# Two more experts in fixed places, a 4 KB descriptor scratch and three more weight buffers in a hybrid GLA, pooling and mixture-of-experts layer

## The chip, the cores and the metric

The kernel runs on one core of a Trainium2 chip. The metric is the device time of one execution in microseconds; a kernel is timed in several runs and the median is compared. Lower is better.

## The reference: what is computed

One transformer layer over 1024 latent tokens of width 1024 with a 256-token context prefix: a modulated RMSNorm, a combined projection into gated linear attention and a pooling branch, an output projection with a gated residual, then a mixture of experts with a gated residual, and a final RMSNorm. What matters here is the mixture of experts. Each token picks one of 4 groups and in it the best 2 of 8 experts:

```python
pg = softmax(t @ w_rg); gp, gi = top_k(pg, 1)                 # one of 4 groups
le = take(t @ w_re, gi); ew, ei = top_k(softmax(le), 2)       # two of its 8 experts
gates = gp * ew / sum(ew)                                     # scattered to (32 experts, tokens)
y = sum_e (silu(t @ wi_a[e]) * (t @ wi_u[e])) @ wo[e] * gates[e][:, None]
```

All is float32. An expert's weights are 1024x512 and 256x1024 (3 MB), 32 experts are 96 MB; 1024 tokens make 2048 (token, expert) pairs.

## The kernel before, in words

**Stages.** Up to about 430 us of the trace come the modulation, the projections, the attention and the pooling (lines 300 to 1057). From line 1266 to 1402 follow the second half of the output projection (`out1_in` and its neighbours), the residual, the norm, and beside them the router (`route`, `counts`, `place`, `tables`). Each finished tile of the normed tokens is stored to `h2_d` in DRAM (L1299), each tile of the residual stream to `x2_d` (L1278). From line 1407 on come the experts, and at the end the last expert block is added on chip to the reloaded residual, normed and stored (L1798 to L1858).

**Blocks.** Every expert gets a number of rows (`CAPS`, by its rank among the experts sorted by load), and experts are put together into blocks of at most 128 rows (`unit`, L1712): 64+64, 96+32 and 64+48 rows from two experts, or 112 to 128 rows of one. There are 19 units and one `merged` block that holds what the two largest experts have over 128 rows, and the smallest's rows. Tokens that fit nowhere would go through a loop after the end (L1861), whose number of turns is read on the chip.

**Fixed places.** The last `NS` experts (26 to 31 before) have no rank by load but a fixed place, 64 rows each, in the first `NS/2` units, so that their weights can be asked for before the router has finished. The other experts' numbers (`eid`) are known only when `order_tables` (L1435) has run; `part` (L1701) reads them into a register of SyncE (`sy.value_load`).

**One block** (class `Block`, L1573): GpSimd gathers its rows from `h2_d` with an indirect DMA for each part (L1590), TensorE transposes them (L1611) and runs the first product (L1626, 8 steps of 128), ScalarE and VectorE apply the gate (L1632, L1633), TensorE transposes (L1639) and runs the second product (L1650), VectorE multiplies by the gates into `y` (L1655), and GpSimd adds `y` into `x2_d` with an accumulating indirect DMA for each part (`scatter`, L1668). All scatters write the same DRAM tensor, so each one waits until the one before it has landed. `y` has two buffers. TensorE's order is written out by hand (L1741 to L1780): the first product of unit n+1, the transposes of unit n+2, then the second product of unit n. `ORDER` is the order of the units.

**Weights.** A weight load is 512 KB into one slab of [128, 1024] floats; an expert needs 4 slabs for the first product and 2 for the second, 192 loads in all, issued by SyncE (L1254). Slabs are taken in turn from the list `slabs` (`next_slab`, L1246), a ring of 39 that reuses the memory of earlier stages: the chunk states (`dS`, `St`), the token buffers (`hall`), a table (`cs`), `wx`, `wraw`, `mix`, `hl`, the weights of the output projection (`woh`, `wol`) and `wz`. A load waits until its slab's last reader is done. SyncE's order isn't written by hand: a list scheduler puts an instruction ahead of others in program order when those aren't ready, so that a load whose slab is free early is issued early.

**The end** (L1782 to L1858). The last unit isn't scattered. When all scatters have landed, SyncE loads `x2_d` into eight slabs `y1` (L1802), TensorE adds the last block's rows by selection matrices `sel` (tag `hl`) from `yp` (tag `wraw`), and the tiles are normed and stored. `fgb`, `y1` and `jk` are the next slabs of the ring.

**GpSimd's scratch.** The program object is made with the default size of GpSimd's DMA descriptor scratch, 16 KB of each SBUF partition.

Of the kernel before, what the change touches and what calls it, by code (L numbers as in the profile page):

```python
# [19 lines left out]
P = 128  # L20
# [4 lines left out]
E = 32  # L25
EPS = 1e-6
NX = 28
NS = 6
ND = E - NS
NP, NA, NQ, NG = NS // 2, 4, 5, 5  # L30
C_X = NS
C_A = C_X + NA
C_B = C_A + NA
# [3 lines left out]
C_Y = C_D + 2  # L37
U_A, U_C, U_S, U_D = NP, NP + NA, NP + NA + NQ, NP + NA + NQ + NG
U_Y = U_D + 2
CAPS = [64] * NS + [32] * 5 + [48] * 5 + [64] * 5 + [80] + [96] * 3 + [112] * 2 + [128] * 3 + [P + 32, P + 64]  # L40
PLACES = [*range(NS), *range(NS, NS + 4), *range(NS + 15, NS + 19), *range(NS + 5, NS + 10),
          *range(NS + 14, NS + 9, -1), *range(NS + 19, E), NS + 4]
ORDER = [0, 1, 2, 13, 3, 14, 7, 15, 4, 8, 17, 18, 5, 9, 12, 10, 16, 6, 11]
NDB = 2
N_W1 = 2
N_W2 = 3
NXB = 3
# [26 lines left out]
def constants():  # L74
# [21 lines left out]
    c[:, O_TOK] = np.arange(P) + 1.0  # L96
    c[:, O_RK:O_RK + E] = PLACES
    c[:, O_CP:O_CP + E] = [CAPS[r] for r in PLACES]
    c[:, O_X:O_X + NX] = np.arange(NX)[None, :]
# [32 lines left out]
def hybrid_layer(ctx, tc, x, c, ctx_in, c_ctx, w_ada, b_ada, norm1_g, w_in, w_decay, b_decay, gla_norm_g,  # L132
                 w_pool, pool_scale, w_out, norm2_g, w_rg, w_re, w_e_in, w_e_out, final_g, cst_d, inv_d, out):
    nc = tc.nc
# [10 lines left out]
    out = out[0]  # L145

    const = ctx.enter_context(tc.tile_pool(name="const", bufs=1))
    dram = ctx.enter_context(tc.tile_pool(name="scratch", bufs=1, space=DRAM))

    kvb_d = [dram.tile([P, 1280], F32, name=f"kvb_d{i}") for i in range(NT)]  # L150
# [9 lines left out]
    cs = early.tile([P, D], F32, name="cs")  # L160
# [33 lines left out]
    def split(hi, lo, src, en=ve):  # L194
        sc.activation(hi, src, AF.Copy)  # L195
        en.tensor_tensor(lo, src, hi.bitcast(F32), OP.subtract)  # L196
# [32 lines left out]
    def mix(i):  # L229
        return mixs[i // 4][:, i % 4]  # L230
# [3 lines left out]
    wst = main  # L234
# [65 lines left out]
    with tc.tile_pool(name="pp", bufs=2) as pp, \  # L300
            tc.manual_schedule(engines={mybir.EngineType.PE, mybir.EngineType.DVE, mybir.EngineType.Activation}):
        xts, wa, wraw, wph, wpl = {}, {}, {}, {}, {}
# [294 lines left out]
    for j in range(5):  # L597
        t = wst.tile([P, D], F32, name="wraw", tag="wraw", bufs=2)
# [51 lines left out]
    St = sd.tile([P, 2, H, P], F32, name="St")  # L650
# [32 lines left out]
    with tc.tile_pool(name="kv", bufs=2) as kv:  # L683
# [115 lines left out]
        with tc.manual_schedule(engines={mybir.EngineType.PE}):  # L799
            k_proj(0, range(8))  # L800
            decay_in(0)
            for n in range(10):
# [18 lines left out]
                if n == 8:  # L821
                    wq, q_steps = load_split(kvw, [(0, 256)], "wk", en=gp)
# [22 lines left out]
    hslab = [hflat[:, j * D:(j + 1) * D] for j in range(10)]  # L845
# [222 lines left out]
    w1p = ctx.enter_context(tc.tile_pool(name="w1p", bufs=1, side="right"))  # L1068
# [165 lines left out]
    def slab(pool, tag, bufs=1):  # L1234
        return pool.tile([P, D], F32, name=tag, tag=tag, bufs=bufs)

    sds = [dS[:, 2 * j:2 * j + 2].rearrange("p i h e -> p (i h e)") for j in range(5)]
    slabs = [sds[4], St.rearrange("p a h e -> p (a h e)"), sds[0], hslab[3], sds[1], *hslab[4:6], sds[2], *hslab[6:8],
             sds[3], *hslab[8:10], cs]
    slabs += [slab(w1p, f"wx{j}") for j in range(N_W1)] + [slab(wst, "wraw", 2) for j in range(2)]  # L1240
    slabs += [mix(j).rearrange("p k n -> p (k n)") for j in range(NT)]
    slabs += [slab(wst, "hl", 2) for j in range(2)]

    ring = [0]

    def next_slab():  # L1246
        ring[0] += 1
        return slabs[(ring[0] - 1) % len(slabs)]

    def wslab(src):  # L1250
# [184 lines left out]
    def order_tables():  # L1435
# [17 lines left out]
        for lo, c in ((0, C_C), (64, C_B)):  # L1453
            c += ORDER[-1] - U_C
            te.matmul(h[lo:lo + 64], lhsT=tT[:, 0, 0:64], rhs=M[:, c:c + 1], start=True, stop=True)
# [13 lines left out]
    def extra_blocks():  # L1469
# [24 lines left out]
        ve.tensor_tensor(er[:, 2], incl, nx, OP.subtract)  # L1494
        ve.tensor_scalar(incl, incl, float(NDB), None, op0=OP.add)
        ve.tensor_copy(nxm, incl[:, E - 1:E])
# [28 lines left out]
        ve.tensor_tensor(poff, poff, fl, OP.add)  # L1525
        ve.scalar_tensor_tensor(poff, poff, float(NDB - 1 + 100), tm, op0=OP.add, op1=OP.mult)
        yield
# [4 lines left out]
        ve.tensor_tensor(slot, slot, q, OP.add)  # L1532
        ve.scalar_tensor_tensor(prk, prk, float(100 - (E - NDB)), sec, op0=OP.add, op1=OP.mult)
        ve.scalar_tensor_tensor(xb, poff, -100.0, prk, op0=OP.add, op1=OP.add)
# [32 lines left out]
        ve.tensor_copy(tab[:, :, 2].bitcast(F32), wtab_x)  # L1567
        ve.tensor_scalar(tab[:, :, 3], xnum, BIG, -NDB * BIG, op0=OP.mult, op1=OP.add)
        extra_tab.append(tab)
# [131 lines left out]
    def part(c, lo):  # L1701

        ev = ND + c if c < NS else lambda: sy.value_load(eid[0:1, c:c + 1], min_val=0, max_val=E - 1)
        return ev, {}, idx[:, c:c + 1], lo, lo + min(CAPS[PLACES[c]], P)

# [6 lines left out]
    def unit(u):  # L1712
        if u < U_A:
            parts = [part(u, 0), part(u + NP, 64)]
        elif u < U_C:
            parts = [part(C_A + u - U_A, 0), part(C_X + u - U_A, 96)]
        elif u < U_S:
            parts = [part(C_C + u - U_C, 0), part(C_B + u - U_C, 64)]
        elif u < U_D:
            parts = [part(C_S + u - U_S, 0)]  # L1720
        else:
            parts = [top[u - U_D]]
        return [Block(parts, wtab[:, u:u + 1])] + [merged] * (u == U_D + 1)

    units = [unit(u) for u in ORDER]
    blocks = [b for u in units for b in u]
# [56 lines left out]
    with tc.manual_schedule(engines={mybir.EngineType.PE, mybir.EngineType.Pool, mybir.EngineType.DVE,  # L1783
                                     mybir.EngineType.Activation}):
        for b in u:
            for j in (4, 5):
                list(b.weights(j))
        for j in range(6):
            list(last.weights(j))
        for b in u:  # L1790
            b.gate_T()
            b.w2()
        fgb = next_slab()
        for h in range(2):
            pt = bank(0, 2, 1)
            spread(pt, fg8, 4 * h)
            sc.activation(fgb[:, h * 512:(h + 1) * 512], pt, AF.Copy)
        y1 = [next_slab() for i in range(NT)]  # L1798
        jk = next_slab()
        sy.dma_start(tab_d, extra_tab[0])  # L1800
        for i in range(NT):
            sy.dma_start(y1[i], x2_d[i * P:(i + 1) * P])  # L1802
        m = last.m
        sel = wst.tile([P, NT, P], F32R, name="hl", bufs=2)
        yp = [wst.tile([P, D], F32R, name="wraw", tag="wraw", bufs=2)[0:m] for k in range(2)]
        for i in range(NT):
            ve.tensor_scalar(sel[:, i], iota, float(i * P), here, op0=OP.add, op1=OP.is_equal)
        for j in range(4):
            last.w1(j)
        last.gate()  # L1810
        last.gate_T()
        y = last.products2()
        for n in range(2):
            ns = slice(n * 512, (n + 1) * 512)
            split(yp[0][:, ns], yp[1][:, ns], y[:, ns])
        pts, ss = {}, {}

        def add(i):

            pts[i] = [bank(5, 3, 7, 6, 4, 0, 2, 1) for n in range(2)]  # L1820
            on_pe = i in PSUM_X2
            for n in range(2 * on_pe):
                te.matmul(pts[i][n], lhsT=ident, rhs=y1[i][:, n * 512:(n + 1) * 512], start=True, stop=False)  # L1823
            for n in range(2):
                ns = slice(n * 512, (n + 1) * 512)
                for k in range(2):
                    te.matmul(pts[i][n], lhsT=sel[0:m, i], rhs=yp[k][:, ns], start=(k == 0 and not on_pe), stop=(k == 1))  # L1827
                if not on_pe:
                    ve.tensor_tensor(y1[i][:, ns], pts[i][n], y1[i][:, ns], OP.add)  # L1829

        def sums(i):

            if i in PSUM_X2:
                return [(pts[i][n], slice(n * 512, (n + 1) * 512)) for n in range(2)]
            return [(y1[i], slice(0, D))]

        def tile_stats(i):
            s = mo.tile([P, 2], F32, name="ss3", bufs=3)
            ss[i] = s[:, 0:1]
            for n, (t, ns) in enumerate(sums(i)):  # L1840
                sc.activation(jk[:, ns], t, AF.Square, scale=D ** -0.5, accum_out=s[:, n:n + 1])
            if i in PSUM_X2:
                ve.scalar_tensor_tensor(ss[i], s[:, 0:1], EPS, s[:, 1:2], op0=OP.add, op1=OP.add)  # L1843
            else:
                ve.tensor_scalar(ss[i], ss[i], EPS, None, op0=OP.add)  # L1845
            gp.tensor_tensor(ss[i], ss[i], mhalf[:, 0:1], OP.pow)  # L1846

        def finish(i):
            for t, ns in sums(i):
                ve.scalar_tensor_tensor(y1[i][:, ns], t, ss[i], fgb[:, ns], op0=OP.mult, op1=OP.mult)  # L1850
            sy.dma_start(out[i * P:(i + 1) * P], y1[i])

        for i in range(NT + 2):
            if i < NT:
                add(i)
            if 0 <= i - 1 < NT:
                tile_stats(i - 1)
            if i >= 2:  # L1858
                finish(i - 2)
    nxv = nc.values_load(nxm[0:1, 0:1], min_val=NDB, max_val=NX)  # L1860
    with tc.For_i(NDB, nxv) as n:  # L1861
        row = mo.tile([P, 4], I32, name="row")
# [46 lines left out]
```

## Time and profile before

| what | value |
|---|---|
| median of 3 runs | 854.39 us (853.29 to 855.78) |
| the profiled execution: its own time | 853.48 us |
| the profiled execution: its span | 851.7 us |
| TensorE busy | 744.7 us, 87% of the span |
| VectorE, ScalarE, GpSimd busy | 432.0, 276.4, 212.8 us |
| DMA moved | 206.84 MB, mean 243 GB/s |

The span is the time between the first and the last recorded instruction; the execution's own time is 1.8 us longer, and the median of the runs is 0.9 us above that. A matmul's end is modelled, so a busy TensorE is not one at its peak. A wait is put down to what was seen to come last.

### The profile page before, as it was taken

To read this page: it belongs to the slowest core of one execution; us is meant where nothing else is said; L and a number is where in the kernel's file an instruction comes from. 1 tells how busy PE (TensorE), PEld (TensorE's weight loads), DVE (VectorE), ACT (ScalarE), POOL (GpSimd) and SP (SyncE) were. 2 spreads that over 40 slices of the span, in tenths; PEclk is the share of its full clock that TensorE was granted. 3 is DMA by queue.
4 is the path that set the end of the run, shared out by engine and by line. 5 is a ranking of instruction groups with operands and counts; after the bars stand their busy time and mean duration, and the time that the engine had idled before them with its cause. 6 is when DMAs were issued, how large, how long until landed. Compare 5 with 4: busy or idle time off the path is not lost. (4 is left out here: it accounts for less than half of the span.)

```text
span 851.7 us, 11806 instructions
## 1 busy us (share of the span) xinstructions
PE 744.7 (87%) x4078; PEld 497.8 (58%) x4078; DVE 432.0 (51%) x884; ACT 276.4 (32%) x525; POOL 212.8 (25%) x201
## 2 busy tenths in 40 slices
PE   4897999989999997879989555999999999989862
PEld 3675788879898976768877442443343433332331
DVE  3547866367785796654466885162232212112144
ACT  4676532344455555343443221210110010010032
POOL 2223000000000204344148553122323321221112
PEclk9999999999999998999999785999998999999987
DMA  9972784253442448554477656999999999999964
GB/s 320 300 261 101 251 277 146 87 163 128 137 143 75 138 134 296 174 189 162 136 233 257 215 200 211 334 366 391 337 374 357 324 325 369 361 358 365 317 242 159
DMA packets 78253, 206.84 MB, mean 243 GB/s; under 512 B 12515, under 2 KB 24919, under 8 KB 78192
## 3 DMA queue, kind: packets, MB, share of 16 engines
q1 hardware_dynamic: 70816, 185.45, 61.3%
q0 software_dynamic: 6624, 18.51, 8.8%
q10 hardware_dynamic: 752, 2.11, 0.7%
q8 instruction: 33, 0.54, 0.2%
q14 instruction: 28, 0.23, 0.1%
HBM read 179.68 MB, written 29.50 MB: 246 GB/s over the span
## 5 line engine op out<-in xcount | busy, mean ns | idle before, releaser
L1668 POOL DMA_INDIRECT x_d<-y,idx x30 | 43.3, 1442 | 166.4 <-DMA x_d<-y,idx 109.1
L1615 DVE COPY hh<-bank 128x512 f32<-128x512 f32 (+1 forms) x20 | 13.4, 668 | 94.0 <-PE bank L1611 93.8
L1655 DVE SCALAR_TENSOR_TENSOR y<-bank,wtab,gtm 128x512 f32<-128x512 f32 (+1 forms) x40 | 29.9, 750 | 48.1 <-PE bank L1650 41.1
L268 PE MATMUL bank<-woh,hh 128*128 128x512 f32 x124 | 52.8, 426 | 0.0
L1641 ACT ACTIVATE gT<-bank 128x256 f32<-128x256 f32 (+1 forms) x20 | 7.4, 375 | 138.7 <-PE bank L1639 138.7
L269 PE MATMUL bank<-wol,hh 128*128 128x512 f32 x124 | 50.2, 404 | 0.8 <-DVE wol L196 0.8
L270 PE MATMUL bank<-woh,hl 128*128 128x512 f32 x124 | 49.9, 402 | 0.1
L1626 PE MATMUL bank<-hall,hh 128*32 128x512 f32 (+3 forms) x152 | 45.8, 620 | 0.0
L268 PE MATMUL bank<-wkh,hh 128*128 128x288 f32 (+1 forms) x144 | 42.7, 297 | 0.0
L270 PE MATMUL bank<-wkh,hl 128*128 128x288 f32 (+1 forms) x144 | 41.9, 291 | 0.1
L269 PE MATMUL bank<-wkl,hh 128*128 128x288 f32 (+1 forms) x144 | 41.7, 290 | 0.0
L196 POOL TENSOR_TENSOR wkl<-wraw,wkh 128x512 fp32r<-128x512 f32 x4 | 6.2, 1548 | 136.2 <-ACT wkh L195 136.2
L1590 POOL DMA_INDIRECT hall<-h_d,idx x32 | 31.5, 984 | 34.3 <-PE bank L1611 10.4
L195 ACT ACTIVATE hh<-hall 128x1024 fp32r<-128x1024 f32 x26 | 27.4, 1055 | 37.9 <-PE bank L269 33.7
L196 DVE TENSOR_TENSOR hl<-hall,hh 128x1024 fp32r<-128x1024 f32 x26 | 31.7, 1222 | 15.5 <-ACT hh L195 15.4
L1626 PE MATMUL bank<-mix,hh 128*64 128x512 f32 (+4 forms) x108 | 39.1, 630 | 0.0
L1626 PE MATMUL bank<-dS,hh 128*32 128x512 f32 (+2 forms) x112 | 38.4, 672 | 0.5 <-DMA dS<-in_w_expert_in_dram 0.5
L268 PE MATMUL bank<-wvh,hh 128*128 128x512 f32 x80 | 32.0, 399 | 0.0
L270 PE MATMUL bank<-wvh,hl 128*128 128x512 f32 x80 | 31.9, 399 | 0.0
L269 PE MATMUL bank<-wvl,hh 128*128 128x512 f32 x80 | 31.9, 399 | 0.0
L405 PE MATMUL bank<-wph,phh 128*128 128x512 f32 x64 | 27.4, 428 | 4.9 <-ACT phh L195 4.2
L1633 DVE TENSOR_TENSOR ga<-ga,bank 128x256 f32<-128x256 f32 (+1 forms) x20 | 8.4, 420 | 42.8 <-ACT ga L1632 42.8
(466 smaller groups left out, 1902.7 us busy)
## 6 DMA issues: line engine op xcount, KB each, us to landing
hall<-in_w_expert_in_dram SPq DMA_DIRECT2D x28, 512.0 KB, 12.8
wat<-in_w_ada_dram SPq DMA_DIRECT2D x24, 512.0 KB, 4.8
mix<-in_w_expert_in_dram SPq DMA_DIRECT2D x23, 512.0 KB, 13.9
dS<-in_w_expert_in_dram SPq DMA_DIRECT2D x18, 512.0 KB, 4.7
mix<-in_w_expert_out_dram SPq DMA_DIRECT2D x17, 512.0 KB, 12.1
wraw<-in_w_ada_dram SPq DMA_DIRECT2D x16, 512.0 KB, 4.3
wol<-in_w_expert_in_dram SPq DMA_DIRECT2D x13, 512.0 KB, 13.3
wraw<-in_w_in_dram SPq DMA_DIRECT2D x12, 512.0 KB, 4.2
```

What stands on the lines that cost most here:

```text
L195: sc.activation(hi, src, AF.Copy)
L196: en.tensor_tensor(lo, src, hi.bitcast(F32), OP.subtract)
L268: te.matmul(dst, lhsT=ah[k], rhs=bh[k], start=(k == ends[0]), stop=False)
L269: te.matmul(dst, lhsT=ah[k], rhs=bl[k], start=False, stop=False)
L270: te.matmul(dst, lhsT=al[k], rhs=bh[k], start=False, stop=(k == ends[1]))
L405: te.matmul(acc[j], lhsT=hh[:, ts], rhs=wph[k], start=(k == 0), stop=False)
L1590: gp.indirect_dma_start(out=self.xg[q], out_offset=None, in_=h2_d, in_offset=ix, bounds_check=D - 1, oob_is_err=False)
L1615: ve.tensor_copy(self.xT[:, 4:8], pt)
L1626: te.matmul(self.ph[q], lhsT=self.xT[:, k, q], rhs=w[:, j * 512:(j + 1) * 512], start=(k == 0), stop=(k == 7))
L1633: ve.tensor_tensor(ga, ga, self.ph[0:m, 256:512], OP.mult)
L1655: ve.scalar_tensor_tensor(y[:, ns], py[n][0:m], self.wt, gtm[0:m, ns], op0=OP.mult, op1=OP.mult)
L1668: gp.indirect_dma_start(out=x2_d, out_offset=ix, in_=y[q], in_offset=None, bounds_check=D - 1, oob_is_err=False, compute_op=OP.add)
```

## The change

`NS` goes from 6 to 8: experts 24 to 31 have fixed places, in four units of 64+64 rows. In return one unit of 64+48 rows from ranked experts goes (`NQ` from 5 to 4), and `CAPS`, `PLACES` and `ORDER` follow; there are still 19 units and the merged block, and 32 scatters. GpSimd's descriptor scratch is set to 4 KB, and the 12 KB per partition that this frees hold three slabs `wq0` to `wq2` in a pool that is open from the start; they head the ring, which has 42 slabs. At the end the ring skips the slabs in `hl` and `wraw` (`kept`) for `fgb`, `y1` and `jk`.

```diff
-NS = 6
+NS = 8
 ND = E - NS
-NP, NA, NQ, NG = NS // 2, 4, 5, 5
+NP, NA, NQ, NG = NS // 2, 4, 4, 5
@@
-CAPS = [64] * NS + [32] * 5 + [48] * 5 + [64] * 5 + [80] + [96] * 3 + [112] * 2 + [128] * 3 + [P + 32, P + 64]
-PLACES = [*range(NS), *range(NS, NS + 4), *range(NS + 15, NS + 19), *range(NS + 5, NS + 10),
-          *range(NS + 14, NS + 9, -1), *range(NS + 19, E), NS + 4]
-ORDER = [0, 1, 2, 13, 3, 14, 7, 15, 4, 8, 17, 18, 5, 9, 12, 10, 16, 6, 11]
+CAPS = [64] * NS + [32] * 5 + [48] * 5 + [64] * 3 + [80] + [96] * 3 + [112] * 2 + [128] * 3 + [P + 32, P + 64]
+PLACES = [*range(NS), *range(NS, NS + 4), *range(NS + 13, NS + 17), *range(NS + 5, NS + 9),
+          NS + 9, *range(NS + 12, NS + 9, -1), *range(NS + 17, E), NS + 4]
+ORDER = [0, 1, 2, 3, 13, 4, 14, 8, 15, 5, 17, 18, 9, 6, 12, 10, 16, 7, 11]
 NDB = 2
+N_W0 = 3
@@
     const = ctx.enter_context(tc.tile_pool(name="const", bufs=1))
+    w0p = ctx.enter_context(tc.tile_pool(name="w0p", bufs=1))
@@
-    slabs = [sds[4], St.rearrange("p a h e -> p (a h e)"), sds[0], hslab[3], sds[1], *hslab[4:6], sds[2], *hslab[6:8],
-             sds[3], *hslab[8:10], cs]
-    slabs += [slab(w1p, f"wx{j}") for j in range(N_W1)] + [slab(wst, "wraw", 2) for j in range(2)]
+    slabs = [slab(w0p, f"wq{j}") for j in range(N_W0)] + [sds[4], St.rearrange("p a h e -> p (a h e)"), sds[0], hslab[3], sds[1],
+             *hslab[4:6], sds[2], *hslab[6:8], sds[3], *hslab[8:10], cs]
+    slabs += [slab(w1p, f"wx{j}") for j in range(N_W1)]
+    raws = [slab(wst, "wraw", 2) for j in range(2)]
+    slabs += raws
     slabs += [mix(j).rearrange("p k n -> p (k n)") for j in range(NT)]
-    slabs += [slab(wst, "hl", 2) for j in range(2)]
+    staging = [slab(wst, "hl", 2) for j in range(2)] + raws
+    slabs += staging[0:2]
@@
+    kept = []
+
     def next_slab():
         ring[0] += 1
+        while any(slabs[(ring[0] - 1) % len(slabs)] is t for t in kept):
+            ring[0] += 1
         return slabs[(ring[0] - 1) % len(slabs)]
@@
             b.gate_T()
             b.w2()
+        kept += staging
         fgb = next_slab()
@@
-    nc = _bacc.Bacc("TRN2", target_bir_lowering=False, num_devices=1)
+    nc = _bacc.Bacc("TRN2", target_bir_lowering=False, num_devices=1, dynamic_dma_scratch_size=4096)
```

## Rows read from the trace of the kernel before

**Rows 1.** The page's table of engines and its forty slices of the span (21.3 us each; a digit is the busy share in tenths), and its line on GpSimd's DMA queue.
```profile
PE 744.7 (87%) x4078; PEld 497.8 (58%) x4078; DVE 432.0 (51%) x884; ACT 276.4 (32%) x525; POOL 212.8 (25%) x201
DMA  9972784253442448554477656999999999999964
...
q0 software_dynamic: 6624, 18.51, 8.8%
```

**Rows 2.** Busy time in stretches from the router's end to the last expert: the stretch, its length, the busy time of PE, PEld, DVE, ACT and POOL with their instructions, the granted clock, the DMA engines' busy share and GB/s.
```profile
510.00:516.00 6.00, 2.13 (x13) 1.06 (x12) 5.83 (x43) 2.34 (x10) 0.77 (x3) 0.50 0.76 262
516.00:520.00 4.00, 1.67 (x14) 1.21 (x15) 3.50 (x24) 0.42 (x3) 2.81 (x8) 0.50 0.01 2
550.00:700.00 150.00, 147.99 (x751) 60.11 (x748) 45.12 (x131) 15.45 (x35) 45.27 (x38) 0.98 1.03 356
700.00:800.00 100.00, 91.65 (x421) 33.35 (x422) 18.32 (x28) 9.10 (x20) 22.14 (x17) 0.98 1.03 363
800.00:810.00 10.00, 7.75 (x32) 2.15 (x30) 2.08 (x9) 0.74 (x2) 1.43 (x1) 1.00 0.75 218
```

**Rows 3.** The instructions of line 1668, the scatters: how many, what GpSimd sat idle for before them (us, times), and the time from issue to landing.
```profile
L1668 POOL DMA_INDIRECT x_d<-y,idx x30: 1314/1432/1602, 556.1 to 810.8; - x30
...
L1668 POOL DMA_INDIRECT x_d<-y,idx_x x2: 1365/1410/1454, 717.2 to 724.0; - x2
...
  DMA x_d<-y,idx: 117.3, 20
...
DMA to landing us min/median/max: 3.9/7.2/10.7
```

**Rows 4.** GpSimd in order of time: start, length, instruction, and in brackets the idle time before it and what ended it. The scatters of the first unit, the one from which several queue up, and the last three (128, 96 and 32 rows).
```profile
556.12 1.49 POOL L1668 DMA_INDIRECT x_d<-y,idx  x1 [5.71 <-DMA hall<-in_w_expert_out_dram]
563.60 1.43 POOL L1668 DMA_INDIRECT x_d<-y,idx  x1 [5.99 <-DMA x_d<-y,idx]
...
707.38 1.59 POOL L1668 DMA_INDIRECT x_d<-y,idx  x1 [5.27 <-DVE y L1655]
...
793.38 1.56 POOL L1668 DMA_INDIRECT x_d<-y,idx  x1 [5.93 <-DMA x_d<-y,idx]
804.09 1.43 POOL L1668 DMA_INDIRECT x_d<-y,idx  x1 [9.14 <-DMA x_d<-y,idx]
810.77 1.33 POOL L1668 DMA_INDIRECT x_d<-y,idx  x1 [5.25 <-DMA x_d<-y,idx]
```

**Rows 5.** The chain that ended last, between 780 and 820 us: start, length, what.
```profile
793.38 9.93 DMA x_d<-y,idx
...
804.09 6.41 DMA x_d<-y,idx
810.50 0.27 issue
810.77 3.85 DMA x_d<-y,idx
...
814.67 3.25 DMA wz<-x_d
```

**Rows 6.** VectorE in order of time: the products with the gates for the last two scattered units and for the last block.
```profile
786.11 1.61 DVE L1655 SCALAR_TENSOR_TENSOR y<-bank,wtab,gtm 128x512 f32<-128x512 f32 x2 [1.91 <-PE bank L1650]
792.76 1.41 DVE L1655 SCALAR_TENSOR_TENSOR y<-bank,wtab,gtm 128x512 f32<-128x512 f32 x2 [5.05 <-PE bank L216]
810.13 1.58 DVE L1655 SCALAR_TENSOR_TENSOR y<-bank,wtab,gtm 112x512 f32<-112x512 f32 x2 [3.84 <-PE bank L1650]
```

**Rows 7.** The page's line on the last kind of weight loads: count, size, median time from issue to landing.
```profile
wol<-in_w_expert_out_dram SPq DMA_DIRECT2D x7, 512.0 KB, 12.7
```

**Rows 8.** SyncE's issues of weight loads in order of time: the last that need no expert number, the first that need one (`wol` at 532.37), and the last nine.
```profile
510.40 1.26 SPq L1254 DMA_DIRECT2D woh<-in_w_expert_out_dram  x2
523.39 1.28 SPq L1254 DMA_DIRECT2D wz<-in_w_expert_out_dram  x3
529.22 0.33 SPq L1254 DMA_DIRECT2D dS<-in_w_expert_out_dram  x1
532.37 1.95 SPq L1254 DMA_DIRECT2D wol<-in_w_expert_in_dram  x4
...
549.24 1.81 SPq L1254 DMA_DIRECT2D hall<-in_w_expert_in_dram  x2
...
786.06 4.11 SPq L1254 DMA_DIRECT2D woh<-in_w_expert_in_dram  x4
791.10 5.06 SPq L1254 DMA_DIRECT2D wol<-in_w_expert_out_dram  x4
```

**Rows 9.** The first gather on GpSimd, the transposes of the first block on TensorE, and the time from issue to landing of all gathers (line 1590).
```profile
518.51 1.11 POOL L1590 DMA_INDIRECT hall<-h_d,idx  x1 [0.73 <-DVE tfin L1390]
...
524.02 1.95 PE L1611 MATMUL bank<-ident,hall 128*128 128x128 f32 x8 [1.57 <-DMA hall<-h_d,idx]
...
DMA to landing us min/median/max: 3.8/7.8/10.2
```

**Rows 10.** The instructions of line 1254 that load into `dS`: the first of them is at 203.8 us.
```profile
L1254 SPq DMA_DIRECT2D dS<-in_w_expert_in_dram x18: 327/333/453, 203.8 to 757.9; - x18
```

**Rows 11.** SyncE at about 59 us, and the same columns as in rows 2 for 60 to 80 us.
```profile
59.31 0.43 SPq L554 DMA_DIRECT2D gnb<-in_gla_norm_g_dram  x1
61.76 0.69 SPq L277 DMA_DIRECT2D bg<-in_b_ada_dram  x1
...
60.00:70.00 10.00, 10.00 (x45) 8.26 (x44) 9.33 (x14) 8.86 (x15) 1.46 (x1) 1.00 0.76 252
70.00:80.00 10.00, 7.32 (x32) 5.53 (x31) 6.55 (x15) 4.65 (x12) 2.73 (x3) 0.83 0.07 26
```

**Rows 12.** TensorE: the second product of one unit of 64+48 rows (one step for each part, at the same time), and VectorE: one of the three steps that make the indices of the fixed experts.
```profile
626.15 0.59 PE L1650 MATMUL bank<-wz,gT 128*48 128x512 f32 x1
626.16 0.59 PE L1650 MATMUL bank<-wol,gT 128*64 128x512 f32 x1
...
517.95 0.17 DVE L1385 SCALAR_TENSOR_TENSOR idx<-bank,tab 128x6 int32<-128x6 f32 x1
```

## The prediction, made before the changed kernel ran

> **What bounds the kernel now.** I read the slices first, then stretches of the expert stage, then GpSimd's timeline and the chain. The slices show that the DMA engines, 20 to 80% busy in the middle, are full from the expert stage on [rows 1], and the stretches that TensorE is full there too: 147.99 of 150 us between 550 and 700, then 91.65 of 100, with the DMA share at 1.03 throughout [rows 2]. Two full resources invite the conclusion that 8 us of starved TensorE (100 less 91.65) are what more buffers would return. The reader should look at a third: GpSimd is busy for a quarter of the span, yet its scatters, 32 with the two of the merged block, wait for one another [rows 3]. From 556.12 to the landing at 814.62 one starts as soon as the last has landed, on average every 8.08 us (258.5/32) [rows 4, 5]. The chain that ended last consists of them and of nothing else before the reload of the residual [rows 5]. VectorE had the rows of the scatter at 793.38 ready at 787.7, those of the next two at 794.2, 10 us before 804.09 [rows 4, 6]. So what ends last is the row of scatters. Up to 707.38 TensorE is level with it: that scatter waits for its `y` [rows 4]. Behind it lie 13 more, and faster matmuls help none of them. A scatter is made of DMA, though: the three last take 10.71, 6.68 and 3.90 us from start to start (the third to the reload), and get shorter as the weight loads run out at about 808 [rows 4, 5, 7].
>
> **The change, part by part.**
>
> *Weights asked for early.* Before, 36 loads need no expert number (6 experts of 6 slabs); the last goes at 529.22, and the four `wol` slabs, last read by the output projection, stay empty until the first number is known at 532.37 [rows 8]. After, 48 loads need none, and the ring of 42 is all filled by such loads: three into `wq` at any time, four into `wol` as soon as `woh` (510.40) [rows 8]. Seven slabs are thus on chip that were not; the two that reuse `wq0` and `wq1` answer to the one at 529.22 and the next. From 549.24 loads follow at DMA's pace, so the lead stays: every load is issued when the seventh after it was issued before. The 192nd goes not at 795.8 (end of the last row, less 0.33) but when the 185th did, at 786.06 [rows 8]; with 12.7 us to landing [rows 7] the loads end at 798.8 in place of 808.5. That is 9.7 us; bounds are 7 us (five slabs, where slabs come free too late at first) and 12.2 (seven at 141 loads in 246.6 us, 1.75 us each [rows 8]).
>
> *What the scatters make of it.* Those up to 793.38 run beside loads as before. That one is beside loads for 5.4 us, half of its 10.71; the rest runs at the pace of a free DMA. No row shows a free scatter of 128 rows: it lies between the 3.90 us of 32 rows and the 6.68 us of 96 rows that still had loads beside them for two thirds [rows 4]. I take 6.0, near the second, for its rows are more like. The step is 5.4+0.5x6.0=8.4, 2.3 less. The next, 6.68, is free throughout: between 3.90 and 6.68, I take 5.5, 1.2 less. The last stays. Sum: **-3.5 us**; with the bounds, -1.5 (loads end at 801.5) to -7.7 (at 796.3, both steps at 3.90).
>
> [...]
>
> *The start of the expert stage.* The four `wol` loads follow the `woh` loads of 510.40; at the pace of the last row of issues (5.06 us for four) they fill the DMA until about 521, where it is empty now from 516 to 520 (share 0.01) [rows 2, 8]. There the first gathers run: the first is issued at 518.51, TensorE's transposes wait for it until 524.02, and all else is behind them [rows 9]. A gather lands in 3.8 us at best and 7.8 in the median, beside loads [rows 9]: the cost is 0 to 4.0. Only the first one or two overlap the tail of the loads, and half the `wol` may go before the last token tile is stored: I take **+0.6**.
>
> *`wq` loads.* SyncE's scheduler brings a load forward to where its slab is free: the first into `dS` goes at 203.8, over 300 us before its use [rows 10]. `wq` is free from the start, so these three may stand at about 59.7, behind the last other load without a condition [rows 11]. Three slabs hold the loads behind them for about 4 us (three at 1.26); the DMA engines have room (0.76, then 0.07 [rows 11]), and the modulation weights behind them have 10 us to spare. Taken as 0; were they placed in the first 45 us, where the DMA is full [rows 1], up to +4.
>
> *Other edits.* A unit of 64+64 rows in place of 64+48 costs TensorE nothing: parts of 64 and 48 take the same 0.59 us beside each other [rows 12]. Six more columns in one table product, and indices 8 wide instead of 6 in steps of 0.17 us [rows 12], are under 0.1 us. Units, scatters and rows are as many as before. Skipping `hl` and `wraw` at the end keeps the reload off slabs that are being used; it starts when the last scatter lands either way.
>
> *The scratch.* No trace row shows GpSimd waiting for room for descriptors; a scatter instruction takes 1.43 us [rows 3]. I take 0, with a bound in the rivals.
>
> **Sum:** -3.5+0.6 = -2.9. The profiled execution took 853.48 (span 851.7, 1.8 around it), 0.9 below the median of the runs; so 850.6 for an execution like it, **851.5** against the median of 854.39.
>
> **Rivals.** *Loads set the end (0.13).* If scatters aren't the limit but follow the loads, the whole 9.7 us return: 854.4-9.7+0.6=845.3. For it speaks starved TensorE after 700 [rows 2]; against it, the `y` that wait 6 to 10 us for their scatter [rows 4, 6].
>
> *The lead is lost at the start (0.20).* The first gathers land beside four `wol` loads like later gathers do, +4.0, and the -3.5 are eaten: 854.9. For: the pause at 516 to 520 is just where they land. Against: half the pause would be left.
>
> *Slower: GpSimd waits for its ring (0.12).* With a quarter of the scratch the same room for descriptors may have to serve several times in the run (6624 packets over 16 engines are 414 for each [rows 1]). If GpSimd then has to look whether room has come free before it writes descriptors, every scatter starts later by x, and since they stand in one row, 32x come on top. From x=0.17 us (5.5/32) the change is slower by 0.3%; at x=0.25 it is +8.0-2.9, 859.5. Against: at most a scatter and a handful of gathers are under way at a time.
>
> [...]
>
> *The change doesn't do what it says (0.03).* The 64 rows of experts 24 and 25 must hold their tokens. The reference's own router gives them 64 and 57 for its inputs, and the ranked experts fit too; with one token more the loop after the end would turn once: a gather (7.8 [rows 9]), a block's loads (12.7 [rows 7]) and a scatter (10.7 [rows 4]) in a row, some +31 us.
>
> **How the numbers follow.** The forecast (0.52) spans -0.5 to -6. A measurement tells 0.3%, 2.6 us, from no change; the sum lies just beyond that, so of the 0.52 about 0.33 count as faster, 0.18 as same. Faster: 0.33+0.13=0.46. Same: 0.18+0.19=0.37. Slower: 0.12+0.03, and 0.02 from the other two: 0.17. The range, 847.0 to 856.0, holds the forecast with its bounds and the lost lead, and leaves out most of the first rival and the slower cases.
>
> **What would show it.** Right: `wq` and `wol` loads issued before 520; the last weight load near 786; scatters back to back until then and steps of 8 and 5.5 us at the end; TensorE without waits for weights after 700; the reload about 3 us earlier. Wrong: a scatter row that isn't back to back before 707, or GpSimd instructions over 1.6 us, a first gather that lands after 524, or a reload that moved by more than 7 us.

## The result

The changed kernel takes 846.73 us (median of 22 runs, 840.67 to 854.65) against 853.2 us of the kernel before beside it; the ratio is 0.9921, 95% interval 0.9900 to 0.9941. Forecast were 851.5 us and -2.9; measured are about -6.7, and 846.73 is 0.3 us below the lower end of the range. The forecast started from 854.39, though; the same ratio makes 847.6 of that, just inside the range, so it is the difference, -6.7 for -2.9, that has to be explained. The change run once more (e10 below) had a ratio of 0.9943, about -4.9. The profiled execution took 848.0 us (span 845.9), 5.8 us of span less than before. Line numbers are 9 higher from the weight loads on (L1263 was L1254), 10 higher from the end stage on; L1677 is the scatter that was L1668.

**The loads.** SyncE's issues of weight loads in the changed kernel, in order of time (start, length, instruction, count):

```profile
62.28 0.39 SPq L1263 DMA_DIRECT2D wq<-in_w_expert_in_dram  x1
...
509.48 1.26 SPq L1263 DMA_DIRECT2D woh<-in_w_expert_in_dram  x2
510.79 2.21 SPq L1263 DMA_DIRECT2D wol<-in_w_expert_in_dram  x4
...
783.75 1.60 SPq L1263 DMA_DIRECT2D mix<-in_w_expert_out_dram  x2
```

The first of the three `wq` loads goes at 62 us (the others follow at 66 and 71), `wol` 22 us earlier than in [rows 8], and the 192nd load goes at 785.02 (forecast 786.06, before 795.82). The stretches (length, busy time of PE, PEld, DVE, ACT, POOL, granted clock, DMA share, GB/s) that answer to [rows 2]:

```profile
510.00:516.00 6.00, 2.18 (x12) 1.10 (x12) 5.79 (x42) 2.24 (x10) 1.61 (x6) 0.50 0.99 350
516.00:520.00 4.00, 1.32 (x13) 1.00 (x13) 3.50 (x28) 0.30 (x2) 2.84 (x5) 0.50 1.01 397
700.00:800.00 100.00, 85.86 (x444) 33.24 (x442) 19.31 (x36) 9.16 (x20) 22.02 (x17) 0.92 0.99 342
800.00:810.00 10.00, 8.55 (x38) 2.69 (x36) 0.42 (x1) 0.74 (x2) 2.72 (x2) 0.96 0.30 44
```

The pause at 516 is filled, and DMA is at 0.30 after 800, where it was at 0.75. TensorE, with more weights at hand, is busy for 6 us *less* between 700 and 800: it now waits behind the scatters. The instructions of line 1677 and who waited for them (us, times) say so; VectorE, which needs a free `y` for TensorE's next results, waited six times. First who waited before the change, when VectorE did not, then the changed kernel:

```profile
who waited for it (us, times):
  POOL x_d L1668: 126.2, 22
```

```profile
L1677 POOL DMA_INDIRECT x_d<-y,idx x30: 1305/1425/1593, 557.4 to 808.4; - x30
...
  DMA x_d<-y,idx: 116.0, 21
...
who waited for it (us, times):
  POOL x_d L1677: 125.1, 23
  DVE y L1664: 53.5, 6
```

**The scatters**, GpSimd in order of time, against [rows 4]:

```profile
557.38 1.49 POOL L1677 DMA_INDIRECT x_d<-y,idx  x1 [4.58 <-DMA dS<-in_w_expert_in_dram]
...
709.08 1.59 POOL L1677 DMA_INDIRECT x_d<-y,idx  x1 [5.24 <-DVE y L1664]
...
794.93 1.56 POOL L1677 DMA_INDIRECT x_d<-y,idx  x1 [5.79 <-DMA x_d<-y,idx]
802.72 1.41 POOL L1677 DMA_INDIRECT x_d<-y,idx  x1 [6.22 <-DMA x_d<-y,idx]
808.40 1.30 POOL L1677 DMA_INDIRECT x_d<-y,idx  x1 [4.27 <-DMA x_d<-y,idx]
```

The chain that ended last, with the reload that answers to [rows 5]:

```profile
794.93 7.01 DMA x_d<-y,idx
...
802.72 5.42 DMA x_d<-y,idx
...
808.40 3.44 DMA x_d<-y,idx
...
811.90 3.25 DMA mix<-x_d
```

The last three steps are 7.79, 5.68 and 3.50 us (forecast 8.4, 5.5, 3.9), 4.3 us less than before in all; up to the scatter at 709.08 the row took 151.70 us, against 151.26 before. The reload stands at 811.90 in place of 814.67: -2.8, where -2.9 was forecast. That this agrees so well is in part luck, as the section on why the prediction was wrong shows. And the reload is not the end of the program.

**The start.** The first gather, and the first transposes, which wait for it, against [rows 9]:

```profile
517.59 1.11 POOL L1599 DMA_INDIRECT hall<-h_d,idx  x1 [0.73 <-DVE tfin L1399]
...
524.46 1.95 PE L1620 MATMUL bank<-ident,hall 128*128 128x128 f32 x8 [2.94 <-DMA hall<-h_d,idx]
```

From the first gather to the transposes it is 6.9 us (5.5 before), and to the first scatter 39.8 (37.6 before).

**The end.** Between VectorE's last operation and the end of the span lay 11.2 us before (840.47 to 851.70) and lie 7.3 us now (838.58 to 845.92). The last output store is issued at 840.49 and 838.60. What stands behind it is an instruction that no busy time counts: GpSimd's DRAIN at the end of the program. First the kernel before: the line's instructions (duration in ns, min/median/max, first and last start), and who SyncE waits for there (us, times, longest):

```profile
L1905 POOLq DRAIN  x3: 46/94/6118, 844.4 to 851.1; - x3
```

```profile
SPq L1905 <- PEq L1905: 6.8, 2, 5.9
```

While it runs, nothing else does (columns as above):

```profile
844.50:850.50 6.00, 0.00 (x0) 0.00 (x0) 0.00 (x0) 0.00 (x0) 0.00 (x0) 0.50 0.01 1
```

Then the changed kernel, the same two views of the line:

```profile
L1915 POOLq DRAIN  x3: 46/94/2402, 842.7 to 845.6; - x3
```

```profile
SPq L1915 <- PEq L1915: 3.1, 2, 2.6
```

One DRAIN took 6.12 us and takes 2.40. SyncE's wait shrinks by the same 3.7 (6.8 to 3.1 us; five engines have semaphore events at that line, so TensorE, named here, need not be the cause: its own DRAINs there last 8 ns). The span's difference is thus +1.26 (first scatter), -4.03 (first scatter to reload), +0.89 (reload to VectorE's last operation) and -3.89 (from there to the end): -5.8.

### The profile page after: what moved, and what is told of

It reads as the page before. It is cut to its first block, busy times and chain, and to the rows that moved or that the text cites. A ratio compares the mean times of both kernels' runs of the same rounds, so it can differ in the third digit from the quotient of the medians.

```text
span 845.9 us, 11767 instructions
## 1 busy us (share of the span) xinstructions
PE 742.8 (88%) x4078; PEld 502.2 (59%) x4078; DVE 428.5 (51%) x884; ACT 276.7 (33%) x525; POOL 211.1 (25%) x201
## 5 line engine op out<-in xcount | busy, mean ns | idle before, releaser
L1677 POOL DMA_INDIRECT x_d<-y,idx x30 | 43.0, 1434 | 161.5 <-DMA x_d<-y,idx 116.0
L1635 PE MATMUL bank<-hall,hh 128*32 128x512 f32 (+4 forms) x156 | 40.9, 611 | 0.0
L1635 PE MATMUL bank<-mix,hh 128*64 128x512 f32 (+3 forms) x132 | 37.7, 600 | 0.0
L1635 PE MATMUL bank<-dS,hh 128*32 128x512 f32 (+3 forms) x88 | 37.2, 640 | 0.0
L1620 PEld LDWEIGHTS bank<-ident,hall 128*128 128x128 f32 (+1 forms) x160 | 22.3, 211 | 15.0 <-issue 15.0
```

Of the source, the lines that this page charges most:

```text
L1620: te.transpose(pt[:, j * m:(j + 1) * m], self.xg[:, k // 2 * 256 + k % 2:(k // 2 + 1) * 256:2], ident[0:m, 0:m])
L1635: te.matmul(self.ph[q], lhsT=self.xT[:, k, q], rhs=w[:, j * 512:(j + 1) * 512], start=(k == 0), stop=(k == 7))
L1677: gp.indirect_dma_start(out=x2_d, out_offset=ix, in_=y[q], in_offset=None, bounds_check=D - 1, oob_is_err=False, compute_op=OP.add)
```

## The experiments

All ratios are to the kernel before. The spans are of one profiled execution each; the first scatter stands anywhere from 554.4 to 560.7 us in them, in kernels with six fixed experts as in those with eight, so the row of scatters is measured from its own start. The columns "to the reload", "to VectorE's last" and "to the end" are lengths (us), each from the event of the column before.

| kernel | fixed experts | slabs | scratch, KB | ratio (95%) | first scatter | to the reload | to VectorE's last | to the end | DRAIN |
|---|---|---|---|---|---|---|---|---|---|
| before | 6 | 39 | 16 | 1 | 556.12 | 258.55 | 25.80 | 11.23 | 6.12 |
| e1 | 6 | 39 | 4 | 0.9975 (0.9948-1.0001) | 554.82 | 258.62 | 25.78 | 6.94 | 2.44 |
| e5 | 6 | 39 | 8 | one run | 554.62 | 258.81 | 26.06 | 7.96 | 3.59 |
| e4 | 6 | 42, `wq` first | 4 | 1.004 (1.001-1.007) | 554.40 | 262.56 | 26.26 | 7.77 | 2.44 |
| e7 | 6 | 42, `wq` last | 4 | 0.9984 (0.9956-1.0012) | 560.72 | 260.67 | 26.70 | 7.30 | 2.44 |
| e2 | 8 | 39 | 16 | 0.996 (0.9934-0.9986) | 555.73 | 256.17 | 25.53 | 10.87 | 6.12 |
| e3 | 8 | 39 | 4 | 0.9951 (0.9925-0.9977) | 557.08 | 255.00 | 25.83 | 6.96 | 2.40 |
| changed | 8 | 42 | 4 | 0.9921 (0.9900-0.9941) | 557.38 | 254.52 | 26.68 | 7.34 | 2.40 |
| e10, changed again | 8 | 42 | 4 | 0.9943 (0.9913-0.9974) | 560.64 | 253.99 | 26.55 | 7.13 | 2.40 |
| e6 | 8 | 42 | 2 | 0.9929 (0.9904-0.9954) | 557.08 | 254.95 | 26.72 | 5.31 | 0.97 |
| e9 | 8 | 42 | 1 | 0.9888 (0.9837-0.9939) | 560.02 | 257.55 | 26.53 | 4.76 | 0.65 |
| e8, late loads cut | 6 | 39 | 16 | 0.9934 (0.9905-0.9962) | 558.47 | 254.03 | 26.61 | 11.15 | 6.12 |
| e11, one scatter less | 8 | 42 | 4 | 0.9886 (0.9829-0.9942) | 556.13 | 247.76 | 25.92 | 7.07 | 2.32 |

### The scratch alone (e1), and at 8 KB (e5)

```diff
-    nc = _bacc.Bacc("TRN2", target_bir_lowering=False, num_devices=1)
+    nc = _bacc.Bacc("TRN2", target_bir_lowering=False, num_devices=1, dynamic_dma_scratch_size=4096)
```

> Only the scratch goes from 16 to 4 KB; six fixed experts and 39 slabs stay. Theory A (the part of the gain behind the last store is the scratch's: GpSimd's DRAIN at the end of the program, 6.12 us before and 2.40 after, gets shorter with it): DRAIN about 2.4 us, scatters and the reload where they were (814.7), the time 3.7 us lower, ratio about 0.9957. Rival B (the end is shorter because the last stores leave from other slabs, or because of the shape of the expert stage): DRAIN 6.1, no change, ratio 1.000. Rival C (a smaller ring makes GpSimd wait): scatters over 1.6 us, slower.

> The kernel before with 8 KB of scratch, for a third point of the DRAIN: 6.12 us at 16 KB and 2.44 at 4 KB. If the DRAIN works through the scratch, its length is linear in the size: 0.307 us per KB and 1.21 us fixed, so 3.67 us. If it is a matter of a threshold, 2.4 or 6.1.

The line's DRAINs, of e1 and then of e5:

```profile
L1905 POOLq DRAIN  x3: 46/94/2443, 842.9 to 845.9; - x3
```

```profile
L1905 POOLq DRAIN  x3: 46/94/3587, 843.0 to 847.2; - x3
```

The scratch alone takes 3.7 us from the DRAIN and nothing from the row of scatters (258.62); the stores still leave from `wz`, `dS` and `hall`. So rival B is out: not the slabs at the end, but the scratch. Rival C too: a scatter instruction takes 1.43 us as before. At 8 KB the DRAIN lies between (3.59, forecast 3.67). So the traces settle what the scratch does to the DRAIN. The times settle less: 0.9975 is -2.1 us, with an interval from -4.4 to 0 that holds -3.7 and, barely, no gain; the second pair, below, shows less still.

### Two more fixed experts without slabs: e2 (16 KB) and e3 (4 KB)

```diff
-N_W0 = 3
+N_W0 = 0
```

This is an edit of the changed kernel; e2 also goes back to 16 KB.

> Eight fixed experts, 39 slabs, 16 KB scratch. Theory A: DRAIN 6.1; the last weight load goes some 5 us earlier than before (four slabs of wol filled early, not seven), the reload at about 813, 1.5 us earlier, ratio about 0.998. Rival B: DRAIN 2.4, and the end after the reload 3 us shorter as in the changed kernel, ratio about 0.9945.

> Eight fixed experts and 4 KB, but without the three slabs (39). Theory A: DRAIN 2.4 and a reload at about 813: 3.7 and some 1.5 us off, ratio about 0.994; what it lacks against the whole change is what three slabs are worth, 1 to 1.5 us. If the gain of the whole change lies in the slabs (rival D), it stays above 0.997.

DRAIN is 6.12 and 2.40: it follows the scratch, not the experts. The last load stands 234.1 and 233.6 us behind the first scatter, where it stood 239.7 before and stands 227.6 in the whole change. The experts thus bring half of the lead in loads, the slabs the other half. In the row of scatters the first 5.6 to 6.1 us of lead take off 2.4 to 3.6 us, more than the 1.5 that I expected, and the next 6 only 0.5 to 2.2 (e2 and e3 against the two traces of the changed kernel).

The times don't confirm all of this. e3 has 0.9951 where the sum of its parts (-3.7 for the DRAIN, -3.6 for the row) would give 0.9914, which lies outside its interval. And e3 against e2, the same kernel with 4 and with 16 KB on one chip, is only -0.8 us in the mean (848.84 and 849.67 us of 12 and 11 runs; a 95% interval of about 2.2 us either way). Together with e1 that makes some -1.5 for the scratch, about 1.5 either way, so that -3.7 lies outside. The DRAIN is 3.7 to 3.8 us shorter in every trace with 4 KB; whether something ahead of it, where executions of one kernel already differ by several us, takes part of that back, no run here shows.

### Three slabs without the experts: `wq` first (e4) and `wq` last in the ring (e7)

e4 is the changed kernel with `NS`, `NQ`, `CAPS`, `PLACES` and `ORDER` of before; e7 also moves the slabs:

```diff
-    slabs = [slab(w0p, f"wq{j}") for j in range(N_W0)] + [sds[4], ...
+    slabs = [sds[4], ...
@@
     slabs += [slab(mo, f"wz{j}") for j in range(N_W2)]
+    slabs += [slab(w0p, f"wq{j}") for j in range(N_W0)]
```

> Six fixed experts, with 4 KB and the three slabs (42). Theory A: DRAIN 2.4; 36 loads without a number fill 36 of 42 slabs, so the wol slabs wait for the router as before, and only three loads' lead is won: reload 1 to 1.5 us earlier, the first scatter where it was (556.1, as no wol loads meet the first gathers), ratio about 0.9945. Rival B: DRAIN 6.1, ratio about 0.9985.

> Six fixed experts, 4 KB, three slabs as in the last run of the first series, which was slower than before by 0.4%, but with the three slabs at the end of the ring. Theory (there the slabs at the head pushed the loads without a number off woh and wol slabs, and DMA stood idle from 510 to 516, share 0.00, while loads for the router's experts held the free slabs): here the first 36 loads go where they go before, the share from 510 to 516 is about 0.4 to 0.8 again, three more loads go at 530 to 535, unit 11's y is ready at about 705 after a first scatter at 555, the reload at about 812.5, ratio about 0.9945. Rival (three more slabs, wherever, put more loads beside the scatters and slow them): mean step of the scatters 8.2 us again, ratio 1.004.

For e4 the expectation missed: it is slower than before, although its DRAIN is 2.44. The same stretches, and SyncE's waits between 509 and 530 us, of e4:

```profile
510.00:516.00 6.00, 2.79 (x22) 1.79 (x22) 5.36 (x38) 1.63 (x7) 2.42 (x9) 0.50 0.00 1
516.00:520.00 4.00, 0.48 (x4) 0.26 (x3) 3.55 (x28) 0.30 (x2) 3.09 (x4) 0.50 0.36 103
```

```profile
SPq L1263 <- DVE dg L1489: 11.6, 1, 11.6
SPq L1712 <- DVE eid L1448: 5.7, 1, 5.7
```

In the order of the program four loads that need a number stand before the last four that need none. With three slabs at the head of the ring three of those four fall on `woh` and one on `wol`, and three of the last ones behind them on `wol`; SyncE issues all seven behind the router (529 to 533). (Waits like these two stand in the other kernels with six fixed experts too, 11.2 to 12.4 us before a load into `wz`; what differs is which loads stand behind them.) DMA, at 0.76 from 510 to 516 before [rows 2], moves nothing (0.00). From 550 to 700 its share is 1.02 to 1.04 in each stretch of the six traces read there (before, changed, e1 to e4), so what isn't loaded by then is missing for good: the rows of unit 11 are ready 154.0 us behind the first scatter in place of 151.0, a delay that the row of scatters keeps.

e7 puts the three at the end of the ring. Unit 11 is back at 151.1, the 3 us of e4 there are gone, and the time is better than e4's by 0.6%, on another chip. So that part of the theory holds. But the gain I expected from three more loads is not there: the row takes 260.67, no less than the 258.6 of e1, and from load 61 on the loads go at about the same distance from the first scatter as in e1 (8.8 us for load 61 in both). The mean step is 8.15, near the rival's 8.2; two steps beside loads (10.89 and 11.15 us, in e1 9.58 and 10.09) make the whole difference, and why they are longer these runs don't tell. What they do tell: slabs alone return nothing. With the two experts' loads to fill them before DMA is full they do shorten the row (by 0.5 to 2.2 us, above). But the first scatter then stands 39.8 to 40.6 us behind the first gather in four traces (changed, e10, e6, e9) and 38.1 in a fifth (e11), 37.7 and 38.1 in e3 and e2, without the slabs. From the first gather to the reload that makes 293.9 to 298.1 us in the four, 292.7 and 294.3 in e3 and e2 (296.2 before): no gain of the slabs is left in the traces, and the ratios (0.9921 and 0.9943, e3 0.9951) don't tell one from none.

### Late loads cut (e8)

```diff
+    nload = [0]
@@
-        sy.dma_start(t, src.rearrange("(p h) n -> p (h n)", h=src.shape[0] // P))
+        v = src.rearrange("(p h) n -> p (h n)", h=src.shape[0] // P)
+        nload[0] += 1
+        if nload[0] > 180:
+            sy.dma_start(t[:, 0:256], v[:, 0:256])
+        else:
+            sy.dma_start(t, v)
```

> The kernel before, in which the last 12 of the 192 weight loads move a quarter of their bytes (the rest of those slabs keeps what was there). Nothing else is changed: same ring, 16 KB. If the last scatters are short because loads have run out, loads that end some 10 us earlier give steps near those of the changed kernel (7.8, 5.7 and 3.5 us in place of 10.7, 6.7 and 3.9) and a reload 3 to 5 us earlier; the DRAIN stays 6.1; ratio about 0.9955. If loads, and not scatters, set the end, the reload comes 8 to 10 us earlier, 0.989. If neither, 1.000.

GpSimd's last scatters in e8:

```profile
795.00 1.56 POOL L1674 DMA_INDIRECT x_d<-y,idx  x1 [5.48 <-DMA x_d<-y,idx]
803.41 1.43 POOL L1674 DMA_INDIRECT x_d<-y,idx  x1 [6.85 <-DMA x_d<-y,idx]
808.92 1.33 POOL L1674 DMA_INDIRECT x_d<-y,idx  x1 [4.08 <-DMA x_d<-y,idx]
```

Steps of 8.41, 5.51 and 3.58 us: fewer bytes at the end, and nothing else, make the last scatters nearly as short as the change does. The row loses 4.5 us of its 258.55, the DRAIN stays at 6.12. If loads set the end, the cut would have returned 8 to 10.

### One scatter left out (e11)

```diff
         def w2(self):
-            self.scatter(self.products2())
+            y = self.products2()
+            if self is not unit12:
+                self.scatter(y)
@@
+    unit12 = units[ORDER.index(12)][0]
```

> The changed kernel without the scatter of unit 12 (one of 112 rows, 25th of the row of 32, about 8 us; its rows never reach the residual). Everything else, its products and its six loads included, stays. Theory (the row of scatters sets the end): the scatters behind it move up by about 8 us, the last two wait for their rows, which are ready at 796, so the reload comes 6 to 8 us earlier and the ratio is about 0.984 to 0.986. Rival (loads or TensorE set the end): the last scatters stay where they are, ratio 0.992.

GpSimd's last scatters, and the reload on SyncE, in e11:

```profile
784.69 1.59 POOL L1679 DMA_INDIRECT x_d<-y,idx  x1 [5.84 <-DMA x_d<-y,idx]
794.29 1.43 POOL L1679 DMA_INDIRECT x_d<-y,idx  x1 [8.01 <-DMA x_d<-y,idx]
800.43 1.31 POOL L1679 DMA_INDIRECT x_d<-y,idx  x1 [4.71 <-DMA x_d<-y,idx]
...
803.89 1.75 SPq L1815 DMA_DIRECT2D mix<-x_d  x4
```

The row is 6.8 us shorter than the changed kernel's, though every load and product is there, and the last load goes at 784.50 (785.02 there). In time it is 843.36 us (4 runs) against 849.28 us of the changed kernel on the same chip (e10). Scatters set the end of the expert stage in the changed kernel too. The ratio, 0.9886, is not as low as the 0.984 to 0.986 that I gave, which left out that this chip gave the changed kernel itself 0.9943.

### Smaller still: 2 KB (e6), 1 KB (e9), and the change again (e10)

```diff
-dynamic_dma_scratch_size=4096)
+dynamic_dma_scratch_size=2048)
```

(1024 in e9.)

> The changed kernel with 2 KB of scratch. Linear DRAIN: 1.82 us, 0.6 us less than at 4 KB, so ratio about 0.9915 against before. Rival (the ring gets too small: a scatter or gather of 128 rows no longer has room beside the one before): scatter instructions over 1.6 us or gaps between scatters, slower than the changed kernel by several us.

> The changed kernel with 1 KB of scratch. DRAIN was 6.12, 3.59, 2.44 and 0.97 us at 16, 8, 4 and 2 KB; if it goes on so, 0.3 to 0.8, some 1.7 us less than at 4 KB: ratio about 0.9915, best of all so far. Rival (below some size GpSimd waits for room): the first gathers, issued every 1.24 us, or the scatters (1.43 us an instruction) take longer, and the row of scatters (254.5 us from the first to the reload) with them; then slower than the changed kernel.

> The changed kernel once more, on the same chip as the run with 1 KB, so that the two can be compared: DRAIN 2.4, 254 to 255 us from the first scatter to the reload, ratio 0.992.

The DRAINs of e6, then of e9:

```profile
L1915 POOLq DRAIN  x3: 46/94/973, 842.3 to 843.8; - x3
```

```profile
L1915 POOLq DRAIN  x3: 46/94/647, 847.4 to 848.6; - x3
```

At 2 KB the DRAIN is shorter than the line through the first points gave (0.97, not 1.82), the scatters keep their 1.42 us and their row its 254.95 us, and the end is 2.0 us shorter than at 4 KB. The median, 845.92, is the lowest but for the runs that leave work out; from 846.73 it can't be told apart. At 1 KB the DRAIN is 0.65, but in its one trace the row takes 257.55 us and the first transposes come 8.1 us after the first gather (6.2 to 7.4 in the others with 8 experts and 42 slabs). Its ratio is better than that of e10 on the same chip, with intervals that overlap. Whether so small a scratch begins to hold GpSimd up stays open; 2 KB is what I would take, by its trace, as its time doesn't tell it from 4 KB.

## Why the prediction was wrong

**The scratch: this step failed.** The prediction took 0, with a loss as the only bound, because it asked one question of the scratch: does GpSimd wait for room? No trace shows that down to 2 KB: a scatter instruction takes 1.42 us in the median there (1.43 at 16 KB), and the row of scatters 254.95 us (254.52 at 4 KB). How the scratch is used, on which the rival of a GpSimd that waits for its ring rested, no run shows. The price lay elsewhere, in a DRAIN at the program's end, 6.12 us that nothing hides. It was in the trace of before, at 844.4, and no part of the sum looked there: the sum went to the reload and treated the 37 us behind it as fixed. Five sizes (6.12, 3.59, 2.44, 0.97, 0.65 us at 16, 8, 4, 2 and 1 KB) and the equal length at 16 KB in three kernels of different shape show that the length goes with the size. From VectorE's last operation to the end it is 10.9 to 11.2 us in the three traces with 16 KB and 6.9 to 7.8 in the seven with 4 KB. With -3.7 for this term the forecast would have been 847.8. Two ends stay open: the times of e1 and of e3 against e2 show less than 3.7 us for the scratch (above), and what the DRAIN does in its time the runs don't say; at 4 KB it is 2.44 us with six fixed experts, 2.40 with eight and 2.32 with one scatter less (e11), so the size is not all.

The 6 us are one instruction of one engine: at the same line of the trace of before the DRAINs of SyncE, VectorE, ScalarE and TensorE take 7 to 17 ns, but for one of 124, and GpSimd's three 46, 94 and 6118 ns.

**The scatters as what ends last: right.** e11 and e8 show it from two sides, and TensorE's 6 us of new idle time with more weights at hand is the same fact. **Their size: nearly right.** Forecast -3.5, measured -4.0 for the row (-4.3 in its last three steps, +0.3 ahead of them), with steps within 0.6 us. The bounds of the free scatter were well placed: 96 rows took 5.42 us to land with next to no loads beside them. The smaller bound was a slip: loads that end at 801.5 and 6.68 us for both steps make -1.0, not -1.5.

**Seven slabs early: right in the sum, with a condition that I did not see.** The last load is 10.8 us earlier (forecast 9.7). But the experts and the slabs are not additive: slabs alone give no lead (e4, e7), experts alone half. And the half that the slabs add is not seen to return time, as said under e7.

**The start: more than forecast, and hidden by luck.** +0.6 was taken. The first transposes stand 6.9 us behind the first gather in place of 5.5 [rows 9], so some 1.4 (0.7 to 2.6 in the other kernels with eight experts and 42 slabs), but only 0.2 to 0.3 in e2 and e3, which fill `wol` too. By the first scatter it is +2.2 us. The reload came out at -2.8 because the first gather happened to stand 0.9 us earlier, which varies by 6 us over these traces: -0.9+2.2-4.0. So the rival of a lead lost at the start came about in part; its 854.9 us did not, nor did the loop after the end turn. **`wq` loads:** they go at 62, 66 and 71 us, where the prediction put them; that they cost nothing is not shown, as the first gather varies by more.

**Not foreseen: +0.9 between reload and VectorE's last operation.** TensorE's restart behind the reload, first of before, then of after (columns as above):

```profile
818.67:822.67 4.00, 4.00 (x8) 1.96 (x7) 0.00 (x0) 0.15 (x1) 0.00 (x0) 0.56 0.99 397
822.67:826.67 4.00, 4.00 (x16) 2.61 (x15) 3.23 (x7) 2.85 (x7) 1.01 (x2) 1.00 0.94 380
```

```profile
815.90:819.90 4.00, 4.00 (x7) 1.96 (x6) 0.00 (x0) 0.04 (x1) 0.00 (x0) 0.50 0.98 384
819.90:823.90 4.00, 4.00 (x13) 2.75 (x13) 2.37 (x5) 2.34 (x6) 0.58 (x1) 0.82 0.96 390
```

The granted clock is about half of full speed when TensorE restarts behind the reload, in both (0.56 and 0.50 in the first rows). Taken as either 0.50 or 1.00, it rises, by its means over these stretches (0.56 is half a us of four at 1.00, 0.82 is 2.6), 7.5 us behind the reload before and 9.4 us in the changed kernel. In four busy us TensorE counts 7 and 8 matmuls at 0.50 and 0.56 and 16 at 1.00; so 1.9 us more at half the clock cost about half of that, an estimate of 0.9 us from these rows, which is the whole difference. e8, with the buffers of before, has it too (26.61 us), and e11, with those of the changed kernel, hasn't (25.92): it isn't tied to a part of the change.

## What to carry to other kernels

Cost a kernel to the last instruction of the trace, not to the last one that counts as busy: what stands there counts too, and here 6 of the 11 us behind VectorE's last operation were one DRAIN, which went from 6.12 us to 0.65 as one size in the program's set-up went from 16 KB to 1. Then measure such a term in the time as well: here the two show different sizes. A larger ring of buffers returned nothing where nothing could be loaded into it while the DMA still had idle time; with such loads the row of scatters got shorter, but it also started later, so count both. And where one row of DMAs sets the end, look at the traffic beside its last members: less of that alone took 4.5 us off the row here (e8).

## What the runs showed of the hardware that was not expected

GpSimd's DRAIN at the end of these programs took 6.12 us with 16 KB of DMA scratch, 3.59 with 8, 2.44 with 4, 0.97 with 2 and 0.65 with 1, and at 16 KB repeated to the nanosecond in three kernels that differ in other things (6118 ns); at 4 KB it was 2443, 2402 or 2321 ns, by kernel. With a scratch of 2 KB, 34 gathers and 32 scatters of up to 128 rows of 4 KB ran as with 4 KB: 0.97 and 1.42 us an instruction in the median at both, and 254.95 us for the row of scatters (254.52 and 253.99).
